# A new order for the attention and recurrence part of a hybrid decoder layer: instructions and loads planned on measured durations, with a term for the port that VectorE and GpSimd share

## The chip, the cores and the metric

The kernel runs on one core of a Trainium2 chip. The metric is the device time of one execution in microseconds (us). One other execution of the kernel before was profiled, and its trace is read below.

## What is computed

One decoder layer on 256 tokens of width 1024 in float32: an input projection, eight attention heads with three branches, four heads of a gated recurrence, an output projection, a layer norm, and then a mixture of 32 experts of which each token uses four.

```python
proj = h @ w_in[l]
(q_a, k_c, v_c, k_s, v_s, k_w, v_w, g_a, q_h, f_h, i_h, g_h) = jnp.split(proj, split_at, axis=-1)
att = nsa_attention(q_a, k_c, v_c, k_s, v_s, k_w, v_w, g_a, positions, ...)
rec = hgrn2(q_h, f_h, i_h, g_h, lbs[l], hg_norm_g[l])
mix = jnp.concatenate([att, rec], axis=-1) @ w_o[l]
h = layer_norm(DN_ALPHA * h + mix, ln1_g[l], ln1_b[l])
ffn = moe(h, w_router[l], b_router[l], w_gate_up[l], b_gate_up[l], w_down[l], b_down[l])
h = layer_norm(DN_ALPHA * h + ffn, ln2_g[l], ln2_b[l])
...
def expert_block(args):
    xb, e = args
    h = xb @ w_gu[e] + b_gu[e]
    gate = jnp.minimum(h[:, :D_FF], SWIGLU_LIMIT)
    up = jnp.clip(h[:, D_FF:], -SWIGLU_LIMIT, SWIGLU_LIMIT)
    act = gate * jax.nn.sigmoid(SWIGLU_ALPHA * gate) * (up + 1.0)
    return act @ w_dn[e] + b_dn[e]
```

An expert's weights are 8 MB of gate and up (`w_gu`) and 4 MB of down (`w_dn`), so the 32 experts bring 384 of these megabytes through the DMA engines.

## The kernel before

**Two parts.** The prefix is all that comes ahead of the experts: projections, recurrence, attention, output projection `out_proj`, layer norm and router `norm_route`, and the first gather of tokens `gather_first`. After it the experts run one behind the other: `gate_up` of expert e, then `down` of expert e-1. Expert weights are read once, from memory, and the prefix is meant to run while the first of them come in.

**Memory.** `Pages` cuts the on-chip memory into 26 pages of 1 MB (8 KB in each of 128 partitions). Two neighbours make a pair; the tile `page6` of a trace or a listing is such a pair, with two pages in it. Weights, activations of the prefix and scratch all live in pages. A page whose last reader is done can be loaded anew. From expert 2 on `pump` loads expert weights by pairs, one DMA of 2 MB for each, and where no pair is whole it waits (`key = pages.get(4096)`); expert 1's `down` weights may still go into single pages. The names are `g0_3` for the fourth page of gate and up of expert 0, `d1_0` for the first page of `down` of expert 1. In its first three experts `gate_up` takes pages in the order that `neighbours` gives: those whose neighbour belongs to the same expert first, then the others.

**Loads.** All loads of the prefix and nearly all of the experts' are issued by SyncE (SP), in one fixed order. A DMA whose page isn't free yet holds back those behind it. `GATE` gives for each load of the prefix the planned time from which it may be put in the queue; since the queue is planned together with the pages, these times also decide which page a load gets.

**Planner.** The prefix is written as some twenty streams (generators), one for `splits`, one for `projections`, `keys`, `queries`, one for each head pair, and so on. `Merge.run` picks the stream that can go on first by the times that `Clock` estimates, and breaks ties by `PRIO`. `Timed` books a cost for every instruction. This happens when the program is built; on the chip each engine runs its instructions in the order that came out, and waits by semaphores. Nearly all instructions of the prefix are issued at one helper line, L147 in this kernel, and the later pair loads at L445.

**Splits.** A float32 product is done as three matmuls on high and low parts (`mm3`). `make_parts` splits a weight unit: ScalarE copies the high part, VectorE or GpSimd subtracts to get the low part; `vec` chooses between these two by their booked times and `POOL_BIAS`. The recurrence needs the gates' running sum `b` (`gates_b`, one scan on VectorE); then six levels (`level_prep`, `levels`) are prepared on VectorE, ScalarE and GpSimd and multiplied on TensorE.

```python
d, p_ = max(clock.at["DVE"], mg.now) + .00104 * n, max(clock.at["POOL"], mg.now) + .0022 * n
return dve if d <= p_ + POOL_BIAS else pool
...
at = {loaded[nm][0][0].key[0]: i for i, nm in enumerate(names)}
return tuple(at[pg] for pg in sorted(at, key=lambda pg: (pg ^ 1 not in at, min(at[pg], at.get(pg ^ 1, 99)), at[pg])))
```

Of the kernel before, what the change touches and what calls it, by code (L numbers as in the profile page):

```python
# [10 lines left out]
F32R = mybir.dt.float32r  # L11
# [28 lines left out]
WARM = 30  # L40
GATE = {'wq0': 2.75, 'wq1': 5.75, 'wkg0': 8.75, 'wkg1': 11.5, 'wgh0': 14.5, 'wgh1': 17.5, 'wqa0': 20.25, 'wqa1': 23.25, 'wvs0': 26.25, 'wkv0': 29.0, 'wc00': 32.0, 'wc10': 35.0, 'wc01': 37.75, 'wc11': 40.75, 'wi0': 43.75, 'wi1': 46.5, 'wo2': 49.5, 'wo3': 61.75, 'wo0': 64.5, 'wo1': 69.75, 'bias': 86.0, 'xres': 87.5, 'ln1': 90.25, 'g0_0': 91.0, 'g0_1': 94.0, 'g0_2': 101.75, 'g0_3': 104.5, 'g0_4': 107.5, 'g0_5': 110.5, 'g0_6': 113.25, 'g0_7': 118.0, 'g1_0': 122.0, 'g1_1': 124.75, 'g1_2': 127.75, 'g1_3': 130.75, 'g1_4': 137.5, 'g1_5': 140.25, 'g1_6': 143.25, 'g1_7': 151.0, 'd0_0': 153.75, 'd0_1': 156.75, 'd0_2': 159.75, 'd0_3': 167.25}
RES = 4
MIX_AT = ('pcT', 'vh')
PRIO = {'splits': 1, 'proj': 50, 'out': 60, 'gates': 10, 'silu': 10, 'levels': 10, 'keys': 8, 'queries': 48, 'comp': 9, 'heads': 4, 'states': 11, 'tables': 3, 'biases': 30, 'sums': 29, 'norm': 3, 'g0': 49, 'g1': 3}
T_TAB = 12.0
POOL_BIAS = -0.5
NHI = 4
NWO = 1
HALVES = 0
UNIT = 2  # L50
KZ_AT = 'ps4'
WC_AT = 6
PARTS = ((4,), (5,), (6, 7))
# [3 lines left out]
SPLIT_2 = (768, 704)  # L57
ORDER = ('f', 'q', 'kg', 'gh', 'qa', 'vs', 'kvc', 'i')

# [12 lines left out]
POLL = "poll"  # L72


class Clock:


    def __init__(self):
        self.at = {e: 0.0 for e in ("PE", "ACT", "DVE", "POOL", "SP", "DMA")}
        self.mem = {}  # L80
        self.same = {}
        self.end = 0.0
        self.tables = None

    def rect(self, ap):
# [29 lines left out]
    def dma(self, outs, ins):  # L115
        x = outs[0]
        t = max([self.at["SP"]] + [self.look(o, True) for o in outs])
        self.at["SP"] = t + .5
        self.at["DMA"] = max(self.at["DMA"], t + 1.5) + int(np.prod(x.shape)) * mybir.dt.size(x.dtype) / 360e3
        self.note(x, self.at["DMA"] + .9, 0.0, "DMA")  # L120

    def run(self, eng, cost, outs, ins, late=.12):
        t = self.at[eng]
        for x in ins:
            t = max(t, self.look(x, False, eng))
        for x in outs:
            t = max(t, self.look(x, True, eng))
        end = t + cost
        self.at[eng] = end
        for x in ins:  # L130
            self.note(x, 0.0, end + late, eng)
        for x in outs:
            self.note(x, end + late, 0.0, eng)
        self.end = max(self.end, end + late)


class Timed:
# [5 lines left out]
    def __getattr__(self, op):  # L143
        f = getattr(self.eng, op)

        def call(*args, **kw):
# [14 lines left out]
            if self.name == "PE":  # L161
                n = size(aps[2])
                if op == "transpose":
                    cost = .11
                elif aps[2].dtype == F32:
                    cost = max(.43 if n < 96 else 0, .00167 * n)
                    if aps[1].ap[1][1] <= 64 and len(aps[1].ap) == 2:
                        cost /= 128 // aps[1].ap[1][1]
                else:
                    cost = max(n, 256) * .00042 if aps[2].dtype == F32R else n * .00042  # L170
            elif self.name == "ACT":
                cost = .1 + .00083 * n + (.1 if "accum_out" in kw else 0)
                fn = args[2] if op == "activation" else None
# [152 lines left out]
def layer(ctx: ExitStack, tc: tile.TileContext, a: dict, out: bass.AP, dbg=None, n_exp=NEXP, cap_limit=CAP):  # L326
# [79 lines left out]
    def pump():  # L406
        while queue and not held_back:
            name, src, shape, kind = queue[0]
            if name == "pk":
                queue.pop(0)  # L410
                sp.dma_start(cst, a["cst"])
                sp.dma_start(pk, a["pk"])
                sp.dma_start(ipk, a["ipk"])
                continue
            whole = kind == "pre" or kind == "small" and shape[2] == 2048
# [1583 lines left out]
```

## Time and profile before

| | |
|---|---|
| median of 3 runs | 1129.42 us (1129.15 to 1130.34) |
| the profiled execution | 1129.57 us, of which its span (first to last instruction) is 1127.4 us |
| TensorE busy | 1052.2 us, 93% of the span |
| VectorE busy | 294.3 us, 26% |
| ScalarE, GpSimd busy | 200.0 us, 75.3 us |
| moved by DMA | 430.02 MB, 381 GB/s over the span |
| TensorE's granted clock, mean | 0.973 |

The shares are means over two very different parts: the prefix, which takes about the first 204 us, and the experts. What a change in the prefix is worth has to be read where the two meet.

### The profile page before, as it was taken

How to read it: one execution, taken by the hardware profiler on the slowest of the kernel's cores; microseconds unless marked ns; L12 is line 12 of the kernel's file. 1: busy time of each engine (PE TensorE's matmuls, PEld its weight loads, DVE VectorE, ACT ScalarE, POOL GpSimd, SP SyncE). 2: the span in 40 equal slices, each digit the busy share in tenths (PEclk: the TensorE clock that was granted, in tenths of full speed). 3: DMA queues.
4: the chain of work that ended last, by engine and by line, in shares of the span. 5: the costliest groups of instructions: out<-in, count | busy, mean ns of one | idle time of the engine just before them, and what ended most of it. 6: DMA issues, size and time to landing. Idle time of an engine off the chain costs nothing. (4 is left out here: it accounts for less than half of the span.)

```text
span 1127.4 us, 13308 instructions
## 1 busy us (share of the span) xinstructions
PE 1052.2 (93%) x5646; PEld 488.3 (43%) x5646; DVE 294.3 (26%) x625; ACT 200.0 (18%) x418; POOL 75.3 (7%) x70
## 2 busy tenths in 40 slices
PE   8888899899999999999998887999999999898986
PEld 8767577443434343434342322434434343332423
DVE  4797985312211111111111010111111111101113
ACT  5566653210101010101010000111101100000101
POOL 4454320000000000000000000000000000000001
PEclk9899899999999999999999997999999899999998
DMA  8842754999999999999999999999999999999992
GB/s 335 330 150 71 281 186 166 425 424 421 421 425 427 427 427 427 427 427 427 427 426 427 423 427 427 427 427 426 426 426 427 427 427 426 427 427 427 427 423 108
DMA packets 35792, 430.02 MB, mean 381 GB/s; under 512 B 3976, under 2 KB 4232, under 8 KB 7056
## 3 DMA queue, kind: packets, MB, share of 16 engines
q1 hardware_dynamic: 34576, 412.33, 87.5%
q10 hardware_dynamic: 1152, 16.78, 3.5%
q8 instruction: 47, 0.77, 0.3%
q14 instruction: 17, 0.14, 0.0%
HBM read 428.05 MB, written 1.05 MB: 381 GB/s over the span
## 5 line engine op out<-in xcount | busy, mean ns | idle before, releaser
L497 PE MATMUL bank<-page,page 128*64 128x512 f32 (+2 forms) x3096 | 693.2, 601 | 32.1 <-SPq L1767 11.8
L497 PEld LDWEIGHTS bank<-page,page 128*64 128x64 f32 (+1 forms) x3096 | 222.8, 139 | 471.4 <-issue 407.1
L1676 DVE TENSOR_SCALAR page<-bank 128x512 f32<-128x512 f32 x32 | 22.1, 692 | 533.9 <-PE bank L497 281.8
L147 PE MATMUL bank<-page,page 128*128 128x256 f32 (+6 forms) x836 | 127.6, 328 | 10.4 <-ACT page L147 5.1
L147 PEld LDWEIGHTS bank<-page,page 128*128 128x128 f32 (+2 forms) x836 | 104.1, 183 | 26.0 <-ACT page L147 7.4
L1677 ACT ACTIVATE page<-page 128x512 f32<-128x512 f32 x32 | 20.2, 630 | 530.5 <-DVE page L1676 530.5
L497 PE MATMUL bank<-page 64*128 64x512 f32 (+2 forms) x260 | 65.8, 608 | 0.9 <-ACT page L1723 0.7
L1658 DVE COPY page<-bank 128x256 f32<-128x256 f32 x32 | 13.6, 425 | 193.6 <-PE bank L497 181.0
L1910 POOL TENSOR_TENSOR page<-page,page 128x320 f32<-128x320 f32 (+1 forms) x2 | 1.6, 794 | 917.9 <-DVE page L1917 917.9
L147 POOL TENSOR_TENSOR page<-page,page 128x512 fp32r<-128x512 f32 (+4 forms) x37 | 55.7, 1521 | 75.6 <-ACT page L147 64.2
L1703 ACT COPY page<-bank 128x512 f32<-128x512 f32 x31 | 18.2, 586 | 229.2 <-PE bank L497 229.2
L497 PE MATMUL bank<-G,page 128*128 128x128 f32 x480 | 57.6, 278 | 0.0
L147 DVE TENSOR_TENSOR page<-page,page 128x512 fp32r<-128x512 f32 (+6 forms) x58 | 49.0, 880 | 27.2 <-ACT page L147 27.1
L497 PEld LDWEIGHTS bank<-G,page 128*128 128x128 f32 x480 | 54.7, 192 | 2.6 <-issue 2.6
L147 ACT CAST page<-page 128x512 fp32r<-128x512 f32 (+3 forms) x71 | 43.5, 654 | 21.4 <-PE bank L147 12.2
L147 PE MATMUL bank<-page 128*128 128x128 f32 (+4 forms) x182 | 34.5, 335 | 9.4 <-DVE page L147 7.0
L497 PEld LDWEIGHTS bank<-page 64*128 64x128 f32 (+1 forms) x260 | 23.3, 186 | 22.8 <-issue 19.2
L147 PEld LDWEIGHTS bank<-page 128*128 128x128 f32 x182 | 27.2, 205 | 13.5 <-DVE page L147 6.1
L1678 DVE TENSOR_TENSOR page<-page 128x512 f32<-128x512 f32 x32 | 22.1, 692 | 22.3 <-ACT page L1677 22.3
L497 PEld LDWEIGHTS <-i 96*64 96x64 bf16 x193 | 8.5, 108 | 39.6 <-issue 39.4
L504 PEld LDWEIGHTS bank<-cst,page 128*128 128x128 f32 x128 | 13.4, 140 | 27.8 <-issue 25.2
L1643 ACT COPY page<-bank 128x512 f32<-128x512 f32 x28 | 16.4, 586 | 43.8 <-PE bank L497 43.8
(150 smaller groups left out, 484.5 us busy)
## 6 DMA issues: line engine op xcount, KB each, us to landing
page<-in_w_gu SPq DMA_DIRECT2D x114, 2048.0 KB, 36.1
page<-in_w_dn SPq DMA_DIRECT2D x55, 2048.0 KB, 35.9
page<-in_w_gu SPq DMA_DIRECT2D x18, 1024.0 KB, 7.1
page<-in_w_gu ACTq DMA_DIRECT2D x5, 2048.0 KB, 28.4
page<-in_w_dn SPq DMA_DIRECT2D x8, 1024.0 KB, 11.7
page<-in_w_dn ACTq DMA_DIRECT2D x3, 2048.0 KB, 28.0
page<-in_w_o SPq DMA_DIRECT2D x4, 1024.0 KB, 5.9
page<-in_w_dl SPq DMA_DIRECT2D x3, 1024.0 KB, 34.3
```

Source lines behind the costliest of these rows:

```text
L147: r = f(*args, **kw)
L497: pe.matmul(o, l, r, start=start, stop=stop, skip_group_check=True)
L504: pe.transpose(o, i_, ident if idn is None else idn)
L1643: act.copy(xg[:, 4 * q:4 * q + 4, :n], bk[0].rearrange("p (a b) -> p a b", a=4)[:, :, :n])
L1658: dve.tensor_copy(sz.rearrange("p a b -> p (a b)"), bk[0][:, :256])
L1676: dve.tensor_scalar(ga, hb[0][:, :n], 7.0, None, OP.min)
L1677: act.activation(sg_, ga, AF.Sigmoid, scale=1.702)
L1678: dve.tensor_tensor(sg_, sg_, ga, OP.mult)
L1703: act.copy(y, py)
L1910: pool.tensor_tensor(z, z, lnp[:, 0, c0:], OP.mult)
```

## The change

The planner's estimates are replaced: DMA at 425 instead of 360 bytes per ns, other costs for float32 and split matmuls, ScalarE and VectorE instructions, and `share`, which lengthens a VectorE instruction by 0.8, and a GpSimd one by 0.25, of the time that both are booked at once. With it come new values for `GATE`, `PRIO`, `RES`, `POOL_BIAS`, `KZ_AT`, `WC_AT` and the order of the projections, where `kg` now stands ahead of `q`. No arithmetic is changed. In the prefix 5 subtractions go from GpSimd to VectorE (61 to 56 and 336 to 341 instructions), and the load of the residual input `xres` is one DMA instead of two (`CUT`).

```diff
-RES = 4
+RES = 3
 MIX_AT = ('pcT', 'vh')
-PRIO = {'splits': 1, 'proj': 50, 'out': 60, 'gates': 10, 'silu': 10, 'levels': 10, 'keys': 8, 'queries': 48, 'comp': 9, 'heads': 4, 'states': 11, 'tables': 3, 'biases': 30, 'sums': 29, 'norm': 3, 'g0': 49, 'g1': 3}
-T_TAB = 12.0
-POOL_BIAS = -0.5
+PRIO = {'splits': 1, 'proj': 8, 'out': 1, 'gates': 10, 'silu': 3, 'levels': 10, 'keys': 3, 'queries': 50, 'comp': 20, 'heads': 3, 'states': 30, 'tables': 9, 'biases': 8, 'sums': 1, 'norm': 60, 'g0': 1, 'g1': 8}
+T_TAB = 11.85
+CUT = 1
+SHARE = {"DVE": .8, "POOL": .25}
+POOL_BIAS = 0.3
...
-ORDER = ('f', 'q', 'kg', 'gh', 'qa', 'vs', 'kvc', 'i')
+ORDER = ('f', 'kg', 'q', 'gh', 'qa', 'vs', 'kvc', 'i')
...
+    def share(self, eng, cost, outs, ins):
+
+        t = self.begin(eng, outs, ins)
+        other = "POOL" if eng == "DVE" else "DVE"
+        both = sum(max(0.0, min(t + cost, b) - max(t, a)) for a, b in self.port[other])
+        cost += both * SHARE[eng]
+        self.port[eng] = self.port[eng][-40:] + [(t, t + cost)]
+        return cost
...
-                    cost = max(.43 if n < 96 else 0, .00167 * n)
+                    cost = max(.3 if n < 96 else 0, .00193 * n)
...
-                cost = .1 + .00083 * n + (.1 if "accum_out" in kw else 0)
+                cost = .17 + .00088 * n + (.1 if "accum_out" in kw else 0)
...
-                cost = .07 + n * (.0065 if op == "reciprocal" else .00104 if two or getattr(aps[1 if len(aps) > 1 else 0].tensor, "_space", None) == PSUM else .00065)
+                far = getattr(aps[1 if len(aps) > 1 else 0].tensor, "_space", None) == PSUM
+                cost = .17 + n * (.0065 if op == "reciprocal" else .00104 if two or far else .00065)
+                shares = not far
...
+            if self.name == "DVE" and shares or self.name == "POOL":
+                cost = self.clock.share(self.name, cost, outs, aps[1:])
```

**The loads around the first experts, on SyncE.** The names are page pairs, `x2048` is one page and `x4096` a pair; `w_gu` is gate and up, `w_dn` is down. Before, from the last pages of expert 1's gate and up to the down weights of expert 1:

```order
L147 DMA page10_76<-in_w_gu 128x2048 x2
L147 DMA page1_1745<-in_w_dn 128x2048 x2
L147 DMA page7_1814<-in_w_dn 128x2048 x2
L147 DMA page11_77<-in_w_gu 128x2048
L147 DMA page4_70<-in_w_gu 128x2048
L445 DMA page6_72<-in_w_gu 128x4096
L445 DMA page8_74<-in_w_gu 128x4096
L445 DMA page0_1322<-in_w_gu 128x4096
L460 DMA page2_1387<-in_w_dn 128x2048 x2
L460 DMA page5_71<-in_w_dn 128x2048 x2
L445 DMA page3_69<-in_w_gu 128x4096
L445 DMA page10_76<-in_w_gu 128x4096
```

And now, from the last two pages ahead of expert 0 (`g2_0` and `g2_1`) on:

```order
L163 DMA page5_1682<-in_w_gu 128x2048 x2
L466 DMA page9_75<-in_w_gu 128x4096
L466 DMA page0_1236<-in_w_gu 128x4096
L466 DMA page6_72<-in_w_gu 128x4096
L481 DMA page3_69<-in_w_dn 128x2048
L481 DMA page10_76<-in_w_dn 128x2048
L481 DMA page2_1266<-in_w_dn 128x2048
L481 DMA page8_74<-in_w_dn 128x2048
L466 DMA page4_70<-in_w_gu 128x4096
L466 DMA page1_1679<-in_w_gu 128x4096
L466 DMA page5_1682<-in_w_gu 128x4096
```

Before, the first three loads behind the prefix take three whole pairs; now two, and the third, `page6`, stands ahead of four single pages.

**Who reads these pages, on TensorE.** Each row is one page half's two matmuls of `gate_up`; a page has two rows, or four where both pages of a pair belong to the expert. Before, the second half of expert 0:

```order
L497 MATMUL bank0_79<-page0_1322,page12_78 64x512 x2
L497 MATMUL bank4_83<-page0_1322,page12_78 64x512 x2
L497 MATMUL bank0_79<-page0_1322,page12_78 64x512 x2
L497 MATMUL bank4_83<-page0_1322,page12_78 64x512 x2
L497 MATMUL bank0_79<-page2_1387,page12_78 64x512 x2
L497 MATMUL bank4_83<-page2_1387,page12_78 64x512 x2
L497 MATMUL bank0_79<-page2_1387,page12_78 64x512 x2
L497 MATMUL bank4_83<-page2_1387,page12_78 64x512 x2
```

Now, the same stretch:

```order
L518 MATMUL bank5_84<-page3_69,page12_78 64x512 x2
L518 MATMUL bank2_81<-page3_69,page12_78 64x512 x2
L518 MATMUL bank5_84<-page10_76,page12_78 64x512 x2
L518 MATMUL bank2_81<-page10_76,page12_78 64x512 x2
L518 MATMUL bank5_84<-page2_1266,page12_78 64x512 x2
L518 MATMUL bank2_81<-page2_1266,page12_78 64x512 x2
L518 MATMUL bank5_84<-page8_74,page12_78 64x512 x2
L518 MATMUL bank2_81<-page8_74,page12_78 64x512 x2
```

Expert 0 had all its eight pages in four pairs (6, 8, 0, 2). Now two of its pairs are whole (9, 0) and four pages are alone (in 3, 10, 2, 8); `page6` holds two pages of expert 1, which `gate_up` of expert 1 reads first.

**VectorE around the scan of the gates.** `TENSOR_TENSOR` with `128x512` or `128x280` into pages 89 and 90 are low parts of splits, `128x1024` by `SCALAR_TENSOR_TENSOR` is the scan that makes `b`, `trig` marks the rotation of the keys. Before:

```order
L147 TENSOR_SCALAR page_77<-page_77,noml 128x256 x4
L147 TENSOR_TENSOR page_89<-page_70,page_89 128x280 x2
L147 SCALAR_TENSOR_TENSOR page_76<-page_76,page_77 128x1024
L147 TENSOR_TENSOR page_90<-page_70,page_90 128x280 x2
L147 TENSOR_TENSOR page_76<-page_76 128x1024
L147 TENSOR_TENSOR page_77<-page_76 128x1024
L147 TENSOR_TENSOR page_89<-page_69,page_89 128x512
```

Now:

```order
L163 TENSOR_SCALAR page_77<-page_77,noml 128x256 x4
L163 TENSOR_SCALAR gat<-bank_81 128x24
L163 TENSOR_SCALAR gat<-bank_82 128x24
L163 TENSOR_TENSOR page_89<-page_69,page_89 128x512
L163 SCALAR_TENSOR_TENSOR page_69<-page_69,page_77 128x1024
L163 TENSOR_TENSOR page_78<-page_77,trig 128x32 x4
L163 TENSOR_TENSOR page_77<-page_78 128x4x8 x2
L163 TENSOR_TENSOR page_77<-page_69 128x1024
L163 TENSOR_TENSOR page_90<-page_70,page_90 128x512
L163 TENSOR_TENSOR page_78<-page_77,trig 128x32 x4
L163 TENSOR_TENSOR page_77<-page_78 128x4x8 x2
L163 TENSOR_TENSOR page_77<-page_77 128x1024
```

The rotation of the keys moved ahead of the levels, and units of `q` (`128x512`) now stand on either side of the scan, where units of `kg` stood.

## Rows read from the trace of the kernel before

**Rows 1.** The page: 40 slices of the span; share of DMA time and GB/s
```profile
DMA  8842754999999999999999999999999999999992
GB/s 335 330 150 71 281 186 166 425 424 421 421 425 427 427 427 427 427 427 427 427 426 427 423 427 427 427 427 426 426 426 427 427 427 426 427 427 427 427 423 108
```

**Rows 2.** The chain that ended last, its last DMA: start, duration, what
```profile
1059.19 39.18 DMA page<-in_w_dn
```

**Rows 3.** Busy time by stretch: PE, PEld, DVE, ACT, POOL, granted clock, DMA share, GB/s
```profile
0.00:190.00 190.00, 165.55 (x1113) 139.16 (x1113) 143.52 (x288) 108.59 (x256) 71.25 (x65) 0.95 0.60 223
190.00:194.50 4.50, 4.50 (x33) 3.79 (x33) 3.27 (x16) 3.02 (x8) 0.00 (x0) 1.00 0.03 7
194.50:1098.00 903.50, 863.68 (x4407) 335.81 (x4406) 138.18 (x304) 83.08 (x146) 0.63 (x1) 0.98 1.00 425
```

**Rows 4.** Timeline of TensorE: gate_up of expert 0, gate_up of expert 1
```profile
204.38 13.90 PE L497 MATMUL bank<-page,page 128*64 128x512 f32 x64
...
222.18 13.90 PE L497 MATMUL bank<-page,page 128*64 128x512 f32 x64
```

**Rows 5.** Timeline of SyncE's DMA issues: start of the first, until the last's end
```profile
194.62 2.00 SPq L147 DMA_DIRECT2D page<-in_w_dn  x4
196.66 1.10 SPq L147 DMA_DIRECT2D page<-in_w_gu  x2
208.03 7.20 SPq L445 DMA_DIRECT2D page<-in_w_gu  x3
216.61 9.54 SPq L460 DMA_DIRECT2D page<-in_w_dn  x4
...
254.06 3.76 SPq L445 DMA_DIRECT2D page<-in_w_dn  x2
```

**Rows 6.** DMA issues by form: count, KB each, median us to landing
```profile
page<-in_w_i SPq DMA_DIRECT2D x2, 1024.0 KB, 4.9
```

**Rows 7.** Busy time by stretch around the first experts, columns as in Rows 3
```profile
194.50:254.00 59.50, 55.25 (x325) 26.01 (x326) 19.16 (x59) 11.74 (x26) 0.63 (x1) 1.00 0.99 412
```

**Rows 8.** TensorE's waits, 6 to 204 us: total, times, longest
```profile
PE bank L147 <- DVE page L147: 13.3, 13, 2.4
PE bank L147 <- ACT page L147: 6.3, 4, 2.4
PE bank L147 <- POOL page L147: 2.7, 3, 1.2
```

**Rows 9.** TensorE's groups by shape, 0 to 204 us: busy, mean ns, idle before
```profile
L147 PE MATMUL bank<-cst,page 128*128 128x128 f32 x98 | 16.7, 296 | 3.8 <-DVE page L147 3.8
...
L147 PE MATMUL bank<-page 128*128 128x128 f32 x96 | 13.7, 303 | 5.5 <-DVE page L147 5.5
...
L147 PE MATMUL bank<-page,page 128*128 128x280 f32 x48 | 10.0, 361 | 3.2 <-ACT page L147 2.4 <-DVE page L147 0.8
```

**Rows 10.** Timeline of TensorE, output projection: the wait for attention's output
```profile
179.42 0.73 PE L147 MATMUL bank<-page,page 128*128 128x512 f32 x2 [1.62 <-ACT page L147]
180.80 5.28 PE L147 MATMUL bank<-page,page 128*128 128x512 f32 x22 [0.64 <-DVE page L147]
```

**Rows 11.** A stretch of the levels at the lower clock, columns as in Rows 3
```profile
87.00:90.00 3.00, 3.00 (x16) 3.00 (x16) 2.96 (x9) 0.00 (x0) 2.03 (x2) 0.50 0.95 314
```

**Rows 12.** Timeline of VectorE around the gates
```profile
22.73 1.29 DVE L147 TENSOR_TENSOR page<-page,page 128x512 fp32r<-128x512 f32 x2
23.94 1.25 DVE L147 TENSOR_TENSOR lbs<-lbe 128x4 f32<-128x4 f32 x1
25.23 0.18 DVE L147 RECIPROCAL lbs<-lbs 128x4 f32<-128x4 f32 x1
...
36.53 2.28 DVE L147 TENSOR_TENSOR_SCAN page<-page,page 128x1024 f32<-128x1024 f32 x1
...
39.43 2.94 DVE L147 TENSOR_TENSOR page<-page 128x1024 f32<-128x1024 f32 x2
```

**Rows 13.** Timeline of GpSimd at the same time
```profile
23.61 2.81 POOL L147 TENSOR_TENSOR page<-page,page 128x512 fp32r<-128x512 f32 x2 [1.05 <-ACT page L147]
```

More of the change, by code (lines that the diff above doesn't have):

```diff
@@ L40 @@
 WARM = 30
-GATE = {'wq0': 2.75, 'wq1': 5.75, 'wkg0': 8.75, 'wkg1': 11.5, 'wgh0': 14.5, 'wgh1': 17.5, 'wqa0': 20.25, 'wqa1': 23.25, 'wvs0': 26.25, 'wkv0': 29.0, 'wc00': 32.0, 'wc10': 35.0, 'wc01': 37.75, 'wc11': 40.75, 'wi0': 43.75, 'wi1': 46.5, 'wo2': 49.5, 'wo3': 61.75, 'wo0': 64.5, 'wo1': 69.75, 'bias': 86.0, 'xres': 87.5, 'ln1': 90.25, 'g0_0': 91.0, 'g0_1': 94.0, 'g0_2': 101.75, 'g0_3': 104.5, 'g0_4': 107.5, 'g0_5': 110.5, 'g0_6': 113.25, 'g0_7': 118.0, 'g1_0': 122.0, 'g1_1': 124.75, 'g1_2': 127.75, 'g1_3': 130.75, 'g1_4': 137.5, 'g1_5': 140.25, 'g1_6': 143.25, 'g1_7': 151.0, 'd0_0': 153.75, 'd0_1': 156.75, 'd0_2': 159.75, 'd0_3': 167.25}
-RES = 4
+GATE = {'wq0': 4.7, 'wkg0': 10.06, 'wq1': 12.64, 'wkg1': 13.3, 'wgh0': 24.25, 'wgh1': 30.59, 'wc10': 35.28, 'wqa0': 35.77, 'wqa1': 39.64, 'wvs0': 40.37, 'wc11': 40.59, 'wo2': 43.9, 'wi0': 45.2, 'wi1': 46.27, 'wc01': 51.06, 'wkv0': 52.5, 'wc00': 54.83, 'wo0': 64.14, 'wo1': 76.05, 'wo3': 76.99, 'bias': 79.47, 'g0_2': 80.61, 'ln1': 84.3, 'xres': 86.45, 'g0_0': 92.84, 'g0_1': 95.46, 'g0_4': 100.86, 'g0_3': 112.78, 'g0_5': 115.04, 'g0_6': 115.93, 'g1_3': 127.76, 'g0_7': 136.39, 'g1_0': 137.34, 'g1_4': 139.34, 'g1_1': 141.34, 'g1_2': 149.42, 'g1_5': 149.89, 'g1_6': 150.2, 'd0_3': 151.43, 'd0_2': 151.74, 'd0_0': 157.31, 'd0_1': 158.35, 'g1_7': 161.63}
+RES = 3
 MIX_AT = ('pcT', 'vh')
-PRIO = {'splits': 1, 'proj': 50, 'out': 60, 'gates': 10, 'silu': 10, 'levels': 10, 'keys': 8, 'queries': 48, 'comp': 9, 'heads': 4, 'states': 11, 'tables': 3, 'biases': 30, 'sums': 29, 'norm': 3, 'g0': 49, 'g1': 3}
-T_TAB = 12.0
-POOL_BIAS = -0.5
+PRIO = {'splits': 1, 'proj': 8, 'out': 1, 'gates': 10, 'silu': 3, 'levels': 10, 'keys': 3, 'queries': 50, 'comp': 20, 'heads': 3, 'states': 30, 'tables': 9, 'biases': 8, 'sums': 1, 'norm': 60, 'g0': 1, 'g1': 8}
[3 more added lines that the diff above has]
+POOL_BIAS = 0.3
 NHI = 4
@@ L50 @@
 UNIT = 2
-KZ_AT = 'ps4'
-WC_AT = 6
+KZ_AT = 'ps2'
+WC_AT = 7
 PARTS = ((4,), (5,), (6, 7))
@@ L83, in __init__ @@
         self.tables = None
+        self.port = {"DVE": [], "POOL": []}
     def rect(self, ap):
@@ L118, in dma, with begin @@
         self.at["SP"] = t + .5
-        self.at["DMA"] = max(self.at["DMA"], t + 1.5) + int(np.prod(x.shape)) * mybir.dt.size(x.dtype) / 360e3
+        self.at["DMA"] = max(self.at["DMA"], t + 1.5) + int(np.prod(x.shape)) * mybir.dt.size(x.dtype) / 425e3
         self.note(x, self.at["DMA"] + .9, 0.0, "DMA")
-    def run(self, eng, cost, outs, ins, late=.12):
+    def begin(self, eng, outs, ins):
         t = self.at[eng]
@@ L127, in run @@
             t = max(t, self.look(x, True, eng))
+        return t
+    def share(self, eng, cost, outs, ins):
[5 more added lines that the diff above has]
+        return cost
+    def run(self, eng, cost, outs, ins, late=.12):
+        t = self.begin(eng, outs, ins)
         end = t + cost
@@ L169, in call @@
                 else:
-                    cost = max(n, 256) * .00042 if aps[2].dtype == F32R else n * .00042
+                    cost = .023 + .00038 * max(n, 256) if aps[2].dtype == F32R else .02 + n * .0004
             elif self.name == "ACT":
-                cost = .1 + .00083 * n + (.1 if "accum_out" in kw else 0)
+                cost = .17 + .00088 * n + (.1 if "accum_out" in kw else 0)
                 fn = args[2] if op == "activation" else None
@@ L413, in pump @@
                 sp.dma_start(ipk, a["ipk"])
+                loaded["pk"] = ([], None)
                 continue
@@ L429, in pump @@
                 loaded[name] = ([bf], bf.v(*shape))
-                for t in range(2):
-                    sp.dma_start(loaded[name][1][:, t], src[:, t])
+                for t in range(0, 2, 2 // CUT):
+                    sp.dma_start(loaded[name][1][:, t:t + 2 // CUT], src[:, t:t + 2 // CUT])
                 continue
@@ L719, in tables @@
     def tables():
+        while "pk" not in loaded:
+            yield POLL
         yield max(T_TAB, clock.ready(pk))
```

## The prediction

> **What bounds the kernel now.** I read the slices of the page first. The DMA row is uneven for the first seven slices and then stands at 9 in each, with 421 to 427 GB/s, until the last slice [rows 1]. The reader is to see two kernels there: a prefix in which the DMA engines have time to spare, and 32 experts that live on what the DMA engines bring. The stretches put numbers to it: 223 GB/s up to 190 us, 7 GB/s from 190 to 194.5 us, and 425 GB/s with a DMA share of 1.00 from 194.5 to 1098 us, while TensorE's matmuls fill 863.68 of those 903.50 us [rows 3]. So TensorE has about 40 us of slack there and the DMA engines have none. The chain of waits says the same: its last weights were issued at 1059.19 us and landed 39.18 us later, which is eight loads of 2 MB in a queue at 4.9 us each; TensorE takes what lands, and what is behind is short [rows 2]. Landing is at 1098.4 us and the span 1127.4 us, so a tail of 29 us follows that the diff doesn't touch.
>
> Therefore two things can move the end, and each moves it one for one: the time at which the stream without holes begins, and holes in it. The time that TensorE needs for an expert can't, short of 40 us. The stream begins when out_proj ends and its pages come free (six single pages from 194.62 us [rows 5]); expert 0's first matmul starts at 204.38 us [rows 4]. I call the latter G. I add up against the profiled execution, 1129.57 us, which is 0.15 us above the median of the three runs shown, 1129.42; span to execution is 2.2 us.
>
> **The loads behind the prefix.** By the listings, 22 pages of 1 MB are on their way when expert 0 begins, before and now. What changes is which pages expert 0 leaves whole. It reads eight pages in 13.90 us, 1.74 us each [rows 4], so a pair is free 3.48 us after its first matmul. Before, the pair loads were issued from 208.03 us, that is G + 3.65, one each 3.6 us for three, then four single pages from 216.61 to 226.15, four more pairs from 229.26 to 243.54, two from 254.06 [rows 5]. From 194.5 to 254 us 412 GB/s were moved in 59.50 us [rows 7], which is 24.5 MB. The six pages, three pairs, four singles and these six pairs are 28 pages, 29.4 MB; the 4.9 MB left take 11.4 us at 427 GB/s, so the last of these 28 leaves the DMA engines at about 265.4 us. At 427 GB/s throughout they need 68.8 us, back to 196.6: the only hole was the 2 us at the start.
>
> Now with G held at 204.38. Only two pairs (9 and 0) come free in expert 0, at 207.9 and 211.3. With the six pages they keep the DMA engines busy for ten pages of 2.46 us, from 196.6 to 221.2 us. The third load wants page6, whose two pages expert 1 reads first, from 222.18 us [rows 4], so it is issued at 222.18 + 3.48 = 225.66. Behind it in SyncE's queue stand the four single pages of expert 1's down weights; their pages are free at about 218.3, when expert 0 ends, but the queue is in order. A lone 1 MB load took 4.9 us from issue to landing [rows 6] where its bytes need 2.46, so 2.45 us pass besides, at the start or the end. The first hole is 225.66 - 221.2 = 4.5 us if they pass at the end, 6.9 if at the start. The page6 pair and the four singles then take 14.7 us, the next two pairs (4 and 1, read by expert 1 too, free as its down or last pages go) 9.8, to 250.1 or 252.6 us; the pair of page5 waits for expert 2, which before was at 254.06 us [rows 5]. Second hole: 3.7 to 3.9 us. Together 8.2 to 10.6 us; neither end is nearer to a row, so I take the middle, **9.4 us lost**. No page frees earlier to give it back, since the slack of the queue that would absorb it (39 us deep at the end) is only built up by the DMA engines themselves.
>
> **When expert 0 starts.** The other term is how much earlier G comes. TensorE's waits from 6 to 204 us are 13.3 us for VectorE, 6.3 for ScalarE and 2.7 for GpSimd [rows 8], 22.3 us in all, so a perfect order could gain that and little more. By stages:
>
> - *Projections to 48 us.* `kg` now comes first. Its units cost 3.2 us of waits [rows 9], which I take as gone. In exchange, units of `q` stand on VectorE behind the scan, 2.28 us, a level's subtraction, 2.94 / 2 = 1.47, and a split's, 1.29 / 2 = 0.65 [rows 12]: 4.4 us that TensorE would wait. Net 1.2 us lost; bounds 3.2 gained (another unit hides it) and 4.4 lost.
> - *Levels, 48 to 90 us.* The products of levels wait 5.5 us for VectorE in 96 matmuls [rows 9]. The rotation of the keys, which VectorE did among the levels' preparation, is now ahead of it. The clock was granted at 0.50 for 3.00 us there, 87 to 90 us, TensorE having waited just before [rows 11]; full speed would give back 1.5 us. I take **7.0 gained**; bounds 0 (VectorE is late anyhow) and 7.0.
> - *Heads, 90 to 179 us.* The transposes wait 3.8 us for VectorE [rows 9]. Here streams are interleaved differently at many places, some freed, some put behind a softmax step. No row prices it; the bounds are all 3.8 gained, or as much lost. I take 0.5 lost.
> - *out_proj and norm.* Its waits, 1.62 and 0.64 us [rows 10], shrink to some 0.6: 1.7 gained. But the norm's sums now all stand behind out_proj on TensorE, where one part lay among it. VectorE's work between 190 and 194.5 us, 3.27 us [rows 3], loses that cover; I take 2.2, of 0 to 3.3. Net 0.5 lost.
>
> Sum 7.0 - 1.2 - 0.5 - 0.5 = **4.8 us earlier**. The bounds don't all fall to one side at once; 2 us later to 12 us earlier is what I allow.
>
> **The five subtractions moved.** A 128x512 one takes 2.81 / 2 = 1.40 us on GpSimd [rows 13] and 0.65 on VectorE [rows 12]: 7.0 us off GpSimd, 3.2 onto VectorE, inside the waits just counted. `xres` as one DMA saves one issue, 1.10 / 2 = 0.55 us [rows 5], on a queue that waits for its gates anyway: nothing.
>
> The trace shows what the two engines do to each other: an addition of 128x4 took 1.25 us from 23.94, while the reciprocal of the same size next to it took 0.18 [rows 12]; it ended at 25.19, when the first of GpSimd's two subtractions from 23.61 was over, at 25.0 [rows 13]. The planner now books 0.8 of such an overlap on VectorE. The Trainium skill, page "SBUF — State Buffer", says that the shared port pair is an exclusive lock, with the other engine blocked for the whole instruction; the row agrees. By the lock, five moved subtractions would free VectorE of up to 7.0 us of blocking for 3.2 us of work; by the planner's 0.8, of 5.6. The difference, 1.4 us, lies within the bounds of the stages.
>
> **Rivals.**
> 1. *Most waits go and few come back, so that expert 0 starts far earlier.* For it: 22.3 us of waits stand there. Against: the new places of `q` and of the norm's sums add waits that I can name. From a lead of 9.4 + 2.3 = 11.7 us the kernel is faster by more than 0.2%, which is about what a measurement can tell. A lead of 14 us gives 1129.6 + 9.4 - 14 = 1125.0 us. Chance 0.25, which takes in the case that the holes are smaller than I say.
> 2. *The two cancel*: lead 7.1 to 11.7 us, 1129.5 us. For it, the levels alone give 7.0. Chance 0.2.
> 3. *The prefix gets nothing*: the waits on VectorE come back at `q` (4.4 us) and the heads (3.8), and eat the 7.0. Lead 0: 1129.6 + 9.4 = 1139 us. Chance 0.17.
> 4. *My forecast*: 1129.6 + 9.4 - 4.8 = 1134.2, say **1134.0 us**, chance 0.38.
>
> **How the numbers follow.** Leads of 12 to -2 us with holes of 8.2 to 10.6 give 1126 to 1142; without the last corner, and reaching halfway into rival 1, 1125.0 to 1141.0 us, outside which I leave 0.18. Faster by over 0.2% (below 1127.2) 0.25, within it 0.2, slower 0.38 + 0.17 = 0.55. The range of the likeliest case alone is 1131.8 to 1137.
>
> **What would show it.** Holes: the profile in stretches from expert 0's first matmul on must show the DMA engines idle some 17 to 24 us behind it, and again about 46 to 50 us behind it; SyncE's third pair load must be issued right when expert 1's second page is read, with the singles right behind. The stream from there must be at 427 GB/s. If there is no hole, the ledger is wrong and the time is about 1124.8 us. The lead: expert 0's first matmul at about 199.6 us. Among the steps, the wait of 5.5 us of the levels' products and the half clock at 87 us should be gone, waits of 2 to 4 us should stand at units of `q` around 36 to 45 us, and out_proj should end later behind its last operand by less than 1 us, with 2 us of idle TensorE in the norm. If expert 0 starts ahead of 193 us, rival 1 holds; after 203, rival 3. The prediction also falls if TensorE, not the DMA engines, turns out late in experts 2 to 31.

## The result, and the profile after

The changed kernel takes 1136.85 us (median of 9 runs, 1131.81 to 1140.19), the kernel before 1130.10 us (9 runs, 1129.15 to 1130.95); the ratio is 1.0051, 95% interval 1.0040 to 1.0062. It is slower by about half a per cent (6.75 us by the medians), and its executions spread over 8.4 us where those of before spread over 1.8. The profiled execution, 1140.19 us, happens to be the longest of the nine.

The page of the changed kernel, engines and slices; they answer to [rows 1]:

```profile
PE 1050.4 (92%) x5646; PEld 489.2 (43%) x5646; DVE 299.7 (26%) x630; ACT 199.2 (17%) x418; POOL 68.0 (6%) x65
...
DMA  8581758499999999999999999999999999999992
GB/s 313 192 340 52 266 195 314 187 370 412 425 428 427 428 426 427 424 428 426 427 428 424 427 426 425 429 425 428 426 426 426 425 428 426 429 424 428 426 423 105
```

The stream at 425 GB/s now begins two slices later: the eighth and ninth, full before, have 187 and 370 GB/s. The stretches show the holes (columns as in [rows 3]):

```profile
194.50:220.00 25.50, 22.05 (x130) 11.60 (x129) 10.73 (x39) 7.30 (x17) 0.63 (x1) 0.93 0.71 288
220.00:240.00 20.00, 19.12 (x86) 6.61 (x88) 4.43 (x11) 1.22 (x2) 0.00 (x0) 0.91 0.59 231
240.00:260.00 20.00, 20.00 (x116) 9.41 (x114) 2.83 (x8) 3.00 (x6) 0.00 (x0) 1.00 0.88 355
260.00:300.00 40.00, 40.00 (x194) 13.65 (x192) 11.85 (x23) 2.41 (x4) 0.00 (x0) 1.00 1.00 426
...
222.00:226.00 4.00, 4.00 (x16) 1.27 (x14) 0.01 (x1) 0.16 (x1) 0.00 (x0) 0.63 0.00 0
...
252.00:256.00 4.00, 4.00 (x22) 1.26 (x18) 0.00 (x0) 0.00 (x0) 0.00 (x0) 1.00 0.43 176
```

From 222 to 226 us nothing moves at all, from 252 to 256 us less than half; from 260 us on the stream is whole. Both holes stand within 2 us of where the prediction put them. A third stretch without loads, 203 to 207 us at 8 GB/s or less, it did not have: here the six pages at the start of the stream were issued from 184.47 us on and had landed at about 204 us, before expert 0 freed its first pair. TensorE, at the start of the two gate_ups, and SyncE's issues (timelines, as in [rows 4] and [rows 5]):

```profile
204.08 13.96 PE L518 MATMUL bank<-page,page 128*64 128x512 f32 x64
...
222.30 15.21 PE L518 MATMUL bank<-page,page 128*64 128x512 f32 x64
```

```profile
207.77 19.81 SPq L466 DMA_DIRECT2D page<-in_w_gu  x3
227.64 2.16 SPq L481 DMA_DIRECT2D page<-in_w_dn  x4
239.50 19.76 SPq L466 DMA_DIRECT2D page<-in_w_gu  x4
```

The first two pair loads go out as expert 0 frees their pages, at 207.77 and 211.21 us; the third goes out at 227.26 us, and the four singles follow by 229.80 us. Expert 1's gate_up took 15.21 us instead of 13.90: the clock was granted at 0.63 from 222 to 226 us, that is partly at the lower level. TensorE had waited 2.41 us for VectorE just ahead of that, but a wait of 2.42 us stands there in the kernel before too, without a drop behind it. Since the third load waits for expert 1's second page, that made the hole longer: it went out 23.2 us behind expert 0's first matmul, where the prediction had 21.3, and no load moved from 219.8 to 228.2 us. In the chain that ended last, the last weights, to hold against [rows 2], land at 1109.28 us:

```profile
1070.10 39.18 DMA page<-in_w_dn
```

That is 10.9 us later than before, and expert 0 started at 204.08 us, against 204.38: in this execution the prefix gained nothing, and the holes cost everything. TensorE's waits in the prefix (6 to 205 us, to hold against [rows 8]) have moved rather than gone:

```profile
PE bank L163 <- DVE page L163: 12.5, 12, 2.8
PE bank L163 <- ACT page L163: 8.1, 9, 3.6
...
PE bank L163 <- POOL page L163: 0.8, 2, 0.6
```

### The profile page after: what moved, and what is told of

It is laid out like the page before. It is cut to its first block, busy times and chain, and to the rows that moved or that the text cites. A ratio compares the mean times of both kernels' runs of the same rounds, so it can differ in the third digit from the quotient of the medians.

```text
span 1138.3 us, 13298 instructions
## 1 busy us (share of the span) xinstructions
PE 1050.4 (92%) x5646; PEld 489.2 (43%) x5646; DVE 299.7 (26%) x630; ACT 199.2 (17%) x418; POOL 68.0 (6%) x65
## 5 line engine op out<-in xcount | busy, mean ns | idle before, releaser
L163 PE MATMUL bank<-page,page 128*128 128x256 f32 (+6 forms) x804 | 127.1, 333 | 11.8 <-ACT page L163 5.3
L163 DVE TENSOR_TENSOR page<-page,page 128x512 fp32r<-128x512 f32 (+5 forms) x64 | 57.9, 943 | 23.1 <-ACT page L163 20.7
L163 POOL TENSOR_TENSOR page<-page,page 128x512 fp32r<-128x512 f32 (+4 forms) x31 | 45.1, 1469 | 91.8 <-ACT page L163 87.4
L163 PE MATMUL bank<-page 128*128 128x128 f32 (+5 forms) x214 | 35.9, 313 | 5.4 <-DVE page L163 4.2
L518 PEld LDWEIGHTS bank<-page 64*128 64x128 f32 (+1 forms) x260 | 23.4, 186 | 22.8 <-issue 19.0
L163 PEld LDWEIGHTS bank<-page 128*128 128x128 f32 (+1 forms) x214 | 28.0, 187 | 9.9 <-DVE page L163 3.9
```

The costliest lines, as they stand in the source:

```text
L163: r = f(*args, **kw)
L518: pe.matmul(o, l, r, start=start, stop=stop, skip_group_check=True)
```

## Experiments

For each run one execution was profiled, so I read it in two parts: **G**, the start of expert 0's first large matmul, and **the rest**, the time of that execution less G. The rest shows the holes and G the prefix. The kernel before has G 204.38 and rest 925.2; the changed one 204.08 and 936.1.

**The changed kernel again.** No edit.

> The changed kernel once more, for a second look at the same prefix and as the partner of the runs that follow. By the ledger of loads: last weights land about 925 + 10.6 us behind expert 0's first matmul whenever that is, so the spread of its times (1131.8 to 1140.2) must come with a spread of expert 0's start of several us, or of the third load's issue. If the spread is in the experts instead, expert 0 starts at 204 us again and the time differs all the same.

1137.63 us (5 runs, 1136.44 to 1139.58), ratio 1.0066 (1.0053 to 1.0079). G 201.81, rest 935.8. So the rest is the same and G moved by 2.3 us, with one and the same program.

**Four whole pairs.** Two pages of expert 0 and two of expert 1 exchange their contents; nothing else is touched.

```diff
+SWAPS = (((0, 0), (1, 0)), ((0, 1), (1, 5)))
...
-            src, shape = a["w_gu"][e, k // 2, :, k % 2 * 2048:...
+            e_, k_ = SWAP.get((e, k), (e, k))
+            src, shape = a["w_gu"][e_, k_ // 2, :, k_ % 2 * 2048:...
...
     mg.run()
+    for (e0, k0), (e1, k1) in SWAPS:
+        x0, x1 = f"g{e0}_{k0}", f"g{e1}_{k1}"
+        loaded[x0], loaded[x1] = loaded[x1], loaded[x0]
```

> The changed kernel with the contents of two pages of expert 0 and two of expert 1 exchanged, so that expert 0 again has four whole pairs; every instruction of the prefix and every load stays where it was. By the ledger: no hole behind expert 0, the execution's time less the start of expert 0 falls from 936.1 to 925 to 926.5 us, so 1126 to 1130 us in all, 10 us under the changed kernel. Rival (the loss lies in the prefix or in the experts' matmuls): no change from the changed kernel's 1136.9 us.

1127.13 us (12 runs, 1121.64 to 1131.26), ratio to the kernel before 0.9970 (0.9956 to 0.9983). G 200.31, rest 924.6. SyncE's issues in this run:

```profile
204.23 7.19 SPq L468 DMA_DIRECT2D page<-in_w_gu  x3
212.81 9.54 SPq L483 DMA_DIRECT2D page<-in_w_dn  x4
225.46 14.28 SPq L468 DMA_DIRECT2D page<-in_w_gu  x4
```

This is the pattern of [rows 5] to within 0.1 us, earlier by 3.8 us. The holes and their whole price come from the pages that the plan gave to expert 0, not from the order of the prefix, and without them the changed kernel is faster than the one before.

**Two pairs broken in the kernel before.** The same exchange, the other way round.

```diff
+SWAPS = (((0, 0), (1, 0)), ((0, 6), (1, 1)))
```

> The kernel before with two pages of expert 0 exchanged for two of expert 1, so that it has two whole pairs and four single pages as the changed kernel has; nothing of its prefix changes. By the ledger: 8.2 to 10.6 us lost, 1138 to 1141 us, two holes at 20 and 48 us behind expert 0's start. Rival: within 2 us of the kernel before.

1137.02 us (5 runs, 1136.74 to 1137.51), ratio 1.0059 (1.0046 to 1.0072). G 205.68, rest 931.1: 5.9 us lost to holes, under the 8.2 that I had set as the least. The listing says why: here 22 pages are loaded ahead of expert 2's first free pair, in the changed kernel 20, before 24.

**Singles allowed.** Expert 2's gate and up may use single pages, so that nothing stands ahead of the free ones.

```diff
-LAX = 1
+LAX = 2
```

> The changed kernel, with expert 2's gate and up also allowed into single pages, so that the third pair no longer stands ahead of the four free single pages. If the loss is that SyncE's queue holds back loads whose pages are free: the first hole goes and 4.5 to 6.9 us come back, 1130 to 1132 us. If the loss is that too few pages can be loaded before expert 2 at all (20 before and behind this edit, against 24 in the kernel before): the holes only move to the stretch ahead of expert 2 and the time stays within 2 us of the changed kernel's.

1139.58 us (5 runs, 1138.80 to 1140.64), ratio 1.0083 (1.0070 to 1.0096). G 201.23, rest 937.6. Two stretches of it:

```profile
220.00:240.00 20.00, 20.00 (x97) 6.42 (x93) 2.77 (x4) 0.63 (x1) 0.00 (x0) 1.00 0.73 289
240.00:260.00 20.00, 20.00 (x118) 9.63 (x118) 2.51 (x7) 3.00 (x6) 0.00 (x0) 1.00 0.74 294
```

SyncE issued the down weights from 213.51 us, 12.3 us behind G, where the changed kernel did so at 227.64, 23.6 behind G; the DMA engines then stood idle later. The queue's order is not the cause.

Not all of this run's rest belongs to expert 0, though. Counted by the bytes moved, its loads run 9.4 us behind those of the kernel before until 400 us behind G (the changed kernel's 10.8 us), and 14.9 us behind from 530 us on: there is one more hole, in the middle of the experts.

```profile
670.00:680.00 10.00, 0.10 (x1) 0.13 (x2) 2.08 (x3) 1.21 (x2) 0.00 (x0) 0.57 0.54 193
...
676.87 0.63 ACT L1700 ACTIVATE page<-page 128x512 f32<-128x512 f32 x1 [38.15 <-issue]
...
679.90 1.08 PE L525 MATMUL bank<-cst,page 128*128 128x128 f32 x4 [12.78 <-DVE page L1704]
```

TensorE waits there for VectorE, and VectorE for an activation on ScalarE, just ahead of which ScalarE issues a load of weights (675.43 us). Two of the runs below, the new durations with the old tables and the plan that knows, have the like hole of some 5.5 us; the other executions have not. Why these three have it stays open.

**Three subtractions off GpSimd.** On the base with whole pairs. The planner books them on GpSimd as before, so all other instructions keep their place.

```diff
+            if self.name == "POOL" and op == "tensor_tensor":
+                MOVED.append(len(MOVED))
+                if MOVED[-1] in (4, 5, 6):
+                    g = getattr(DVE[0], op)
-            r = f(*args, **kw)
+            r = g(*args, **kw)
```

> The run with the four whole pairs, and three of GpSimd's 128x512 subtractions (two at 24.0 us, one at 32.6 us) issued on VectorE at the same place of the program; nothing else moves. If the shared port is what makes the angles, the scaling of the gates and the scan slow (1.2 instead of 0.2 us, 2.8 instead of 1.1, 3.4 instead of 2.3), VectorE loses 3 x 0.65 us of work and gains some 4 us of blocking: the last matmul of q and kg ends 2 to 3 us earlier (49.4 to about 47 us) and the time is 1124 to 1126 us against 1127.1. If VectorE is simply the busier engine, 2 us later: 1127 to 1129 us.

1126.69 us (12 runs, 1125.63 to 1129.71), ratio 0.9968 (0.9959 to 0.9977). G 201.57. q and kg end at 48.1 us instead of 49.4: 1.3 us, half of what I expected, and the time shows no difference from the base. Even the 1.3 us need not be the port's: from 30 to 50 us TensorE's granted clock was 0.91 in this execution and 0.74 in that of the base.

**All two-input work of the prefix off GpSimd.** The condition above becomes `if True`.

> The same base with every two-input instruction of GpSimd in the prefix issued on VectorE at its place, some 55 us of GpSimd's time, 26 us of work for VectorE. If the port is held as a whole by one engine at a time, VectorE gets back the blocking: its busy time in the first 190 us does not rise by more than 5 us (150.8 us in the changed kernel), and the executions spread by less than 2 us, since nobody races for the port; time 1122 to 1130 us. If the two engines work side by side, VectorE's busy time rises by about 26 us and the time to 1135 us or more. If the spread stays near 10 us, the port is not its cause.

1115.38 us (4 runs, 1111.84 to 1117.70), ratio 0.9873 (0.9857 to 0.9889). G 187.19, rest 924.7. The pages of the base and of this run, engines:

```profile
PE 1047.6 (93%) x5646; PEld 487.9 (43%) x5646; DVE 299.1 (27%) x630; ACT 199.0 (18%) x418; POOL 69.4 (6%) x65
...
PE 1036.6 (93%) x5646; PEld 479.7 (43%) x5646; DVE 290.9 (26%) x668; ACT 199.1 (18%) x418; POOL 11.4 (1%) x27
```

VectorE took over 38 instructions and is busy 8.2 us less; GpSimd gave up 58.0 us. So VectorE got back more than the work cost, as the first expectation says. The time is 11.8 us under the base and under the range that I had set, and the spread, 5.9 us in four runs, did not shrink as I expected.

How that becomes 11.8 us is not all told by VectorE. Up to G (columns as in [rows 3]; base, then this run):

```profile
0.00:200.31 200.31, 178.06 (x1213) 152.12 (x1215) 158.22 (x333) 114.99 (x275) 65.93 (x61) 0.94 0.64 243
...
0.00:187.19 187.19, 169.47 (x1214) 144.29 (x1216) 149.98 (x371) 115.06 (x275) 7.94 (x23) 1.00 0.68 260
```

G fell by 13.1 us. Only 4.5 of these are idle time of TensorE (22.25 to 17.72 us); 8.6 are busy time: the same matmuls, at a granted clock of 1.00 instead of 0.94. Its waits for VectorE went from 7.1 to 6.7 us only. In the base the clock stood at 0.50 five times in the prefix, the first two times in or right behind waits of TensorE of 3.26 and 2.92 us; here the longest wait is 1.91 us and it never fell. The profiled execution is also the fastest of the four, 3.5 us under their median, with the highest mean clock. Whether the free port kept the clock up by making the waits short, or it was up for another reason, no run tells.

**The ten beside the levels alone.** The condition is `MOVED[-1] in range(9, 19)`.

> The run with four whole pairs, and only the ten subtractions of GpSimd from 47.8 to 78 us, those beside the levels, issued on VectorE. The forecast had 7 us of gain in the levels that did not come. If the port is what held it back: q and kg end at 49.4 us as they did, the last level's products at 82 to 86 us instead of 90.7, and the time is 1120 to 1124 us against 1127.1. If VectorE is the bound there with or without the port: 89 us or later, 1126 to 1129 us.

1125.76 us (5 runs, 1125.07 to 1126.43), ratio 0.9957 (0.9944 to 0.9970). G 199.49; q and kg end at 49.3 us, the last level at 87.8. That is between the two expectations: 3 us are gained at the levels, of which up to 1.7 can be the clock (1.00 from 48 to 90 us against 0.96), and 1.4 us are left at the end. The spread is 1.4 us.

**The same on the kernel before**, all of it, and then from GpSimd's eighth subtraction on (`MOVED[-1] >= 7`).

> The kernel before, its order and its pages, with every two-input instruction of GpSimd in the prefix issued on VectorE at its place. If the port is what holds the prefix in either order, expert 0 starts at 190 to 196 us instead of 204.4 to 205.7 and the time is 1115 to 1122 us. If the gain of the like run on the changed kernel came from its new order, which freed VectorE at the right places, less than 4 us: 1126 us or more.

> As the last run on the kernel before, but the first seven of GpSimd's subtractions, up to 22 us, stay on GpSimd, since on VectorE they stood behind an instruction that waits for a load until 21.8 us and held TensorE up by 5 us. If the port holds the prefix in the old order too, that 5 us is what hid it: expert 0 starts at 198 to 201 us and the time is 1123 to 1127 us. If the old order has no use for the freed VectorE, 1129 to 1132 us as in the last run.

All: 1130.33 us (11 runs, 1127.07 to 1133.83), ratio 0.9999 (0.9988 to 1.0010), G 205.37. From the eighth on: 1126.16 us (6 runs, 1122.16 to 1128.16), ratio 0.9959 (0.9945 to 0.9973), G 201.79. TensorE in the first of these runs:

```profile
22.83 17.67 PE L155 MATMUL bank<-page,page 128*128 128x256 f32 x131 [4.77 <-DVE page L155]
```

VectorE waits for the load of `pk` until 21.8 us, and the subtractions that I had put on it stood behind that. Left on GpSimd, they cost nothing there, and 4 us remain of the gain. So the old order has use for a free VectorE too, with a third of the new one's gain in time; in TensorE's idle time up to G the two are near each other, 26.28 to 22.68 us here and 22.25 to 17.72 us there.

**Parts of the tables.** q ahead of kg again in the changed kernel; then the new durations with all the old tables.

```diff
-ORDER = ('f', 'kg', 'q', 'gh', 'qa', 'vs', 'kvc', 'i')
+ORDER = ('f', 'q', 'kg', 'gh', 'qa', 'vs', 'kvc', 'i')
```

> The changed kernel with the units of q ahead of those of kg again, as in the kernel before; the planner then lays out pages and loads anew, so the execution's time is read in two parts. If putting kg first is what costs the 4 us by which q and kg end later (45.7 us before, 49.4 to 50.7 now), they end at 45 to 47 us and expert 0 starts at 196 to 200 us. Rival: the order of the two makes no difference, and they end at 49 to 51 us. Pages: three whole pairs come free in expert 0 by the listing, so the rest behind expert 0's start is 926 to 931 us.

> The planner's new durations and its term for the port with all of the old tables (GATE, PRIO, RES, bias, order, CUT). If the new durations alone give the earlier start, expert 0 starts at 200 to 202 us; if the tables were needed, at 204 us or later. Three pairs are whole in expert 0 by the listing; behind its start 925 to 931 us. 1126 to 1134 us in all.

The first: 1145.99 us (4 runs, 1142.70 to 1147.40), ratio 1.0129 (1.0110 to 1.0148), G 215.67, rest 931.2. The second: 1140.03 us (6 runs, 1138.55 to 1142.44), ratio 1.0089 (1.0075 to 1.0104), G 210.10, rest 928.6. Both times lie above what I expected. The rest of the first fits the 22 pages that it loads ahead of expert 2's first free pair; that of the second holds the late hole told above. The new durations without the new tables start expert 0 6 us later than before, and the new tables with one entry turned back 11 us later. What q and kg cost can't be read from the first, since its whole plan is another: a small edit moves the plan by more than the change under study did.

**A plan that knows.** `POOL_BIAS = 1000.` lets the planner give its splits and levels to VectorE itself; one page exchanged for whole pairs.

> The changed kernel with a bias under which the planner itself gives all splits and levels to VectorE and plans the order for it, with one page of expert 0 and one of expert 1 exchanged so that four pairs are whole. If a plan that knows is better than a plan made for GpSimd's help and run without it (1115.4 us), 1108 to 1114 us; if the order matters little beside the port, 1113 to 1117 us; if the new plan is unlucky elsewhere (as with q ahead of kg, 1146 us), above 1120 us. Behind expert 0's start 924.5 to 926 us in each case.

1129.57 us (12 runs, 1127.49 to 1133.20), ratio 0.9993 (0.9982 to 1.0003), G 200.26, rest 927.3. GpSimd kept 20.8 us of work, and the plan is 14 us worse than that of the changed kernel run without GpSimd. Its rest lies above the expected 926; the late hole told above is what the trace shows for it. Its G is 13 us later than in that run although VectorE does nearly all the work here too, with a granted clock of 0.97 and 23.75 us of idle TensorE up to G. So a free port alone does not give that run's gain.

## Why the prediction was right, and where not

**Direction and range** hold: 1136.85 us lies between 1125 and 1141, and the sign is that of two terms which fight as I said. The size, 6.75 us slower by the medians where 4.6 were forecast, is off in both terms, and the lead came out near by luck, as told below.

**The term of the holes** was 9.4 us, of 8.2 to 10.6. The rests say 10.9 and 10.6 us in two executions of the changed kernel (936.1 and 935.8 less 925.2), and the medians with and without whole pairs differ by 9.7 to 10.5. So the upper end came out, where a load's 2.45 us pass at its start; but a part of it is the third load's later issue, which the prediction did not have.

**Its mechanism** I told wrongly in one point. I made it a matter of SyncE's queue, which holds back four free pages. With single pages allowed they were not held back, and nothing was won. What counts is how many pages can be loaded at all until expert 2 frees its first pair. In the kernel before that is 49.7 us behind G, and the stream begins 7.8 us ahead of G, so 57.5 us have to be filled, at 2.46 us a page 23.4 pages. Twenty-four suffice. Twenty-two leave 1.4 pages or 3.4 us, and with one start of 2.45 us 5.9; measured 5.9, and 6.0 in the run with q ahead of kg. Twenty leave 3.4 x 2.46 = 8.4 us, and with one start 10.8; measured 10.6 and 10.9. I made this count when most of the numbers were known, and it is good to 2 us, not to a tenth: in the changed kernel expert 2 freed its first pair only 51.4 us behind G, since expert 1's gate_up ran partly at the lower clock, and with that the count gives 12.5; with single pages allowed it gives 10.8 where the loads were 9.4 us late. The four that the changed kernel lacks are single pages whose neighbours are in use, which no pair load can take; the singles allowed to expert 2 alone leave the loads of expert 3 waiting for pairs, so that the count stays at twenty. The sum came out nearly right because it counted these pages in, though the words around it blamed the queue.

**The term of the lead** was 4.8 us, of -2 to 12. Four executions with this prefix gave 0.3, 2.6, 4.1 and 3.2 us; the medians of the kernel before and of the one with whole pairs give 1130.42 - 1127.13 = 3.3. The prefix of before varies too: it gave G 204.38 and 205.68. That the lead is within 1.5 us of the forecast is luck: three of the four stages below are off by 2 to 6 us each, and the errors cancel. I matched TensorE's rows of each trace with the program's order one by one; the ends of stages in us:

| end of | before | changed | again | whole pairs | singles | no GpSimd |
|---|---|---|---|---|---|---|
| q and kg | 45.7 | 50.7 | 49.5 | 49.4 | 49.9 | 44.5 |
| vs (levels done) | 96.3 | 100.6 | 95.4 | 95.3 | 98.1 | 85.4 |
| start of out_proj | 164.0 | 162.5 | 160.0 | 160.0 | 160.8 | 146.8 |
| G | 204.4 | 204.1 | 201.8 | 200.3 | 201.2 | 187.2 |

The last column is the fastest of that run's four executions, 3.5 us under their median.

- *Projections*: forecast 1.2 us lost, measured 3.7 to 5.0. This term was mis-sized. The wait at `q` stood where I put it, but it came in two pieces, 3.64 us for ScalarE and 2.85 for VectorE:

```profile
33.02 0.50 PE L163 MATMUL bank<-page,page 128*128 128x256 f32 x2 [3.64 <-ACT page L163]
...
41.24 2.51 PE L163 MATMUL bank<-page,page 128*128 128x256 f32 x10 [2.85 <-DVE page L163]
...
62.73 2.05 PE L163 MATMUL bank<-page 128*128 128x128 f32 x16 [1.63 <-DVE page L163]
...
67.57 2.02 PE L163 MATMUL bank<-page 128*128 128x128 f32 x16 [1.40 <-DVE page L163]
...
96.74 0.63 PE L163 MATMUL bank<-cst,page 128*128 128x128 f32 x4 [2.44 <-DVE page L163]
...
179.54 5.28 PE L163 MATMUL bank<-page,page 128*128 128x512 f32 x22 [0.37 <-DVE page L163]
...
195.80 0.69 PE L163 MATMUL bank<-page 128*128 128x96 f32 x4 [1.12 <-ACT page L163]
```

The piece on ScalarE begins on VectorE. These are its rows, and GpSimd's at the same time:

```profile
25.10 1.23 DVE L163 SCALAR_TENSOR_TENSOR ang<-nlo,ang 128x24 f32<-128x24 f32 x1
26.37 1.22 DVE L163 SCALAR_TENSOR_TENSOR ang<-turns,ang 128x24 f32<-128x24 f32 x1
...
33.60 3.38 DVE L163 TENSOR_TENSOR_SCAN page<-page,page 128x1024 f32<-128x1024 f32 x1
```

```profile
25.00 2.54 POOL L163 TENSOR_TENSOR page<-page,page 128x512 fp32r<-128x512 f32 x2 [2.12 <-ACT page L163]
...
33.56 1.28 POOL L163 TENSOR_TENSOR page<-page,page 128x512 fp32r<-128x512 f32 x1 [3.20 <-ACT page L163]
```

Two angles of 128x24 took 1.2 us each beside GpSimd's two subtractions. ScalarE's sine waited for them, and its copies for `q` stand behind the sine. Without GpSimd the same angle took 0.18 us, the scan 2.28, and TensorE's wait at that place was 0.92 us:

```profile
24.38 0.18 DVE L173 SCALAR_TENSOR_TENSOR ang<-turns,ang 128x24 f32<-128x24 f32 x1
...
30.89 2.28 DVE L173 TENSOR_TENSOR_SCAN page<-page,page 128x1024 f32<-128x1024 f32 x1
```

```profile
30.30 0.50 PE L173 MATMUL bank<-page,page 128*128 128x256 f32 x2 [0.92 <-ACT page L173]
```

The waits are not the whole of it. The sum had no term here for TensorE's granted clock. From 30 to 50 us (columns as in [rows 3]) before, changed and without GpSimd:

```profile
30.00:50.00 20.00, 16.19 (x93) 14.11 (x91) 15.93 (x30) 11.75 (x26) 7.97 (x7) 0.83 0.89 360
...
30.00:50.00 20.00, 13.91 (x76) 13.51 (x77) 15.76 (x30) 11.79 (x25) 5.89 (x5) 0.74 0.32 108
...
30.00:50.00 20.00, 16.35 (x119) 15.03 (x120) 19.17 (x37) 13.47 (x26) 0.00 (x0) 1.00 0.51 183
```

In the changed kernel the clock fell in or right behind each of the two waits at `q`; 0.74 instead of 0.83 over 20 us is up to 1.8 us of the 3.7 to 5.0.

- *Levels*: forecast 7.0 us gained, measured 0.7 to 4.7 (from the end of q and kg to that of vs). This is the step that failed: I had the waits for VectorE go with the rotation of the keys, and in the changed kernel's first execution they came back at 62.7, 67.6 and 96.7 us, 1.4 to 2.4 us each; in the second and with whole pairs one of 2.9 us at 71.8 us was left, with a fall of the clock behind it. Without GpSimd's work, TensorE is 10.9 us ahead of the kernel before at the end of vs, of which up to 5.1 us is the clock (0.50 for 10.2 us until then in the kernel before, never there); with only the ten instructions beside the levels moved it gained 3 us at the last level. So the port is a likely cause of these waits, and the only one that I tried, but its share is not measured apart from the clock's.
- *Heads*: forecast 0.5 us lost, measured 3.0 to 5.8 gained (from vs to out_proj); no row had priced it, and its bound of 3.8 was too narrow.
- *out_proj and norm*: forecast 0.5 us lost, measured from 0.1 gained to 1.4 lost. Its wait fell to 0.37 us, and TensorE waits 1.12 us in the norm. The two executions that lost here had a granted clock of 0.91 from 185 to 205 us, the two others 1.00.

**Rivals.** The third, no lead, is what the profiled execution shows; the median lies between it and the forecast. The first, a far earlier start, was seen only without GpSimd's work, with the clock at 1.00 throughout: there G is 187.2 us.

**What stays open.** Why the changed kernel's executions spread by 8 us is shown only in part (below). Both the port and TensorE's clock differ between executions of one program, and no run held either fixed. The run without GpSimd's work still spread by 5.9 us in four, so the port isn't all of it; its four times follow the mean granted clock (0.990 for 1111.84 us, 0.980 for 1117.70), without a sign of which causes which.

## What to carry to other kernels

Where a stream of loads has to be without holes, count the pages that can be loaded until the next ones come free, and look at which free pages the loads can't use; the layout that a planner leaves behind can be worth more than its order of instructions. Here an exchange of two pages of one expert for two of the next gave back 10 us and turned a loss of 0.5% into a gain of 0.3%. Before work is shared out between VectorE and GpSimd, try it without GpSimd, in the same order of all else: the gain depends on the order, and is not there in each (0, 4 and 12 us in three runs). And look at TensorE's granted clock before the gain is booked: of the 13.1 us by which expert 0 started earlier in the best of them, 8.6 were matmuls at a higher clock.

## What the runs showed of the hardware

GpSimd's help cost VectorE more than it saved: with 38 instructions more VectorE was busy 8.2 us less in the new order, and with 43 more 4.7 us less in the old one (294.3 to 289.6 us). The Trainium skill, page "SBUF — State Buffer", section "SBUF: two separate sides", says that whichever of the two engines starts first holds the shared pair for its whole instruction. The traces agree that one engine is held up until the other is done, and show in one program that is run twice that it need not be the same one. First VectorE and GpSimd in the changed kernel, then both in its second execution, at the same instructions:

```profile
58.59 1.78 DVE L163 TENSOR_TENSOR page<-page 128x512 f32<-128x512 f32 x1
60.30 2.38 DVE L163 TENSOR_TENSOR page<-page,page 128x512 f32<-128x512 f32 x1
```

```profile
58.36 1.46 POOL L163 TENSOR_TENSOR page<-page,page 128x512 fp32r<-128x512 f32 x1 [5.62 <-ACT page L163]
59.79 2.34 POOL L163 TENSOR_TENSOR page<-page 128x1024 f32<-128x1024 f32 x1
```

```profile
57.39 0.68 DVE L163 TENSOR_TENSOR page<-page 128x512 f32<-128x512 f32 x1
57.99 0.67 DVE L163 TENSOR_TENSOR page<-page,page 128x512 f32<-128x512 f32 x1
```

```profile
57.16 2.67 POOL L163 TENSOR_TENSOR page<-page,page 128x512 fp32r<-128x512 f32 x1 [5.62 <-ACT page L163]
59.79 3.68 POOL L163 TENSOR_TENSOR page<-page 128x1024 f32<-128x1024 f32 x1
```

In the first, each of VectorE's two additions ends 0.55 us behind the GpSimd instruction beside it; they end at 62.68 us, 4.1 us after the first began, and the next level's products wait for them. In the second, VectorE got through with 0.68 and 0.67 us, and it is GpSimd's instructions that are long, 2.67 and 3.68 us. There the third level's products began 3.0 us earlier (59.73 instead of 62.73 us), of which 1.2 us stood already at the second level's (53.85 instead of 55.05 us). So which engine is held up can change from execution to execution, and the time with it. What decides it the rows don't tell: in both, GpSimd's first instruction starts 0.23 us ahead of VectorE's first addition, while VectorE's subtraction before that still runs (to 58.66 and 57.46 us). The run with whole pairs and the one with singles allowed went as the second did.

The row that the prediction read bears the hold out more closely than it said. It had GpSimd's first subtraction end at 25.0 us, half of a row of two; that subtraction itself took 1.56 us, to 25.17, 0.02 us ahead of the end of the addition that it held up.
